# A head's fourth key and query class, the root of one column, and the last row in halves: three small edits to a hybrid decoder block

## The chip, the cores and the metric

The kernel runs on one core of a Trainium2 chip. The metric is device time in microseconds of one execution, the median of several. The engines are named as in the profile: PE (matrix multiply) with its weight loads, DVE (vector), ACT (activations and copies), POOL (elementwise work on a second vector engine) and SP, whose queue issues most DMAs. Every engine works through its instructions in order and waits on semaphores for the others.

## The reference, cut to what matters

One decoder layer on a sequence of 2048 positions with width 1024: an adaptive RMS norm, one wide input projection, two branches in parallel (a gated linear recurrence and a dilated attention), a gated merge, an output projection, and a last RMS norm. The part that the change touches is the attention and the last norm:

```python
DILATED_GROUPS = ((128, 1), (512, 4), (2048, 16))      # window, dilation; 8 heads of width 128
for window, dilation in DILATED_GROUPS:
    o, l = dilated_window_attention(q, k, v, window, dilation)   # banded softmax over strided keys
    outs.append(o); lses.append(l)
w = jax.nn.softmax(jnp.stack(lses, axis=0), axis=0)    # the three mixed by their denominators
o = jnp.einsum("gbsh,gbshd->bshd", w, jnp.stack(outs, axis=0))
...
x = x + gate[:, None, :] * (merged @ w_o[l])
return rms_norm(x, g_final)                            # x * rsqrt(mean(x*x) + 1e-6) * g
```

All matrix products are computed in three passes: each operand is split into a high part (rounded) and a low part (the rest), and high times high, high times low and low times high are summed. A split is therefore two instructions: a copy that rounds (mostly ACT, line 160) and a subtraction that gives the rest (POOL, line 166, or DVE, line 169).

## The kernel before, in words

The program runs in stages: input projections with a Strassen scheme (to about 1340 us), the attention together with the projections of the branches' outputs (about 1350 to 1866 us), the rest of these projections (to about 1965 us and on), and the output projection with the last norm (from about 2010 us).

**Attention.** The sequence is handled in two halves of 1024 positions (`f`), and each half has eight heads; I number these 16 in program order from 0 to 15. Positions are sorted by their remainder modulo 4 into four classes. A head has six units of work, `ORDER`: class 0, window part 0, class 1, window part 1, class 2, class 3. A class unit takes the queries of one class against the keys of the same class; a window unit takes the queries of 512 neighbouring positions, which are spread over all four classes.

Time is laid out in slots, one unit of scores in each (lines 1881 to 1906). A slot has five places: HEAD, the scores and their softmax, SOFTMAX, two thirds of the slot's filling work, EXCHANGE, the last third, WEIGHTS, the transposes of the unit seven slots back, then the sums of the unit eight slots back, TAIL. The filling work (`fill`) is the matrix product of the branches' outputs, some 2.8 steps of three 512-column matmuls for each slot, so that PE has work while the softmax goes on. The order in which the instructions are written is the order in which each engine runs them (`manual_schedule`); what stands at a place is put there by `at(slot, place, function)`.

For a head that starts in slot B, `Head.enlist` (line 1696) sets these steps, as far as they matter here:

- `load_kq` (line 1418), one DMA on SP's queue for each class, 256 KB in the first half and 384 KB in the second, into one of four buffers `kraw`: classes 0 and 1 in slot B-5, class 2 in B-4, class 3 in B-3, all at TAIL. For the first head all four are loaded in slot -5.
- `split_kq` (line 1425): ACT writes the high half into `KQ[:, 0, c]`, POOL the low half into `KQ[:, 1, c]` (DVE for classes 0, 1 and 3 of the first head). `KQ` has one buffer, so the split of a class has to follow the last scores of the head before that read it. Class 0 is split at B-2 HEAD, class 1 at B-2 SOFTMAX, class 2 at B-1 HEAD, class 3 at B HEAD. The scores of class 3 of the head before stand in slot B-1.
- `window_queries` (line 1430): POOL copies the queries of a window part, high and low, from all four classes into the order of the window unit (tile `q1`; its rows read `CAST q<-kq`). Part 0 at B HEAD, for the scores in slot B+1; part 1 at B+1 EXCHANGE.
- `gather` (line 1626) at B-1 WEIGHTS, for the head before: four small ACT instructions that spread that head's softmax statistics; then `exchange` (line 1633), one small PE product of these (row `sc<-sm,msk`) in the middle of the scores of slot B; then `maxima` on DVE, `exponentials` on ACT, and `weights` on DVE at B WEIGHTS, whose result `M` scales the exponentials on ACT (line 1542) ahead of the transposes, from slot B+1 on.
- `split_v` and `split_v1` (lines 1446 and 1463): the values of an older head, high on ACT, low on POOL, at TAIL; that of the class 3 unit stands at B-1 TAIL.

**The end.** The output projection handles the rows in eight pairs of blocks (`output_pair`, line 2085), each with seven products; two rows of 128 positions come out of a pair, and each is normalised: square sums on ACT (`square`, line 2018), the root by `rstd_first` and `rstd_last` or `mean_first`, `mean_last` and `rstd_last`, then a scale and a store. `rstd_last` (line 176) takes the reciprocal of ACT's square root and improves it by one Newton step, five DVE instructions on a tile of 128 x 1 in this stage (128 x 4 elsewhere). In the last pair the gain has been multiplied in before; the second row is scaled whole on ACT (line 2141) and stored by one DMA of 512 KB, just ahead of the first row's last product (`last_output`, line 2045), whose square sum, root, scaling in two halves (ACT and DVE) and two DMAs of 256 KB end the program.

Of the kernel before, what the change touches and what calls it, by code (L numbers as in the profile page):

```python
# [14 lines left out]
AF = mybir.ActivationFunctionType  # L15
ALU = mybir.AluOpType
# [9 lines left out]
CH = 512  # L26
# [64 lines left out]
def decoder_block(ctx, tc, x, c, positions, g_norm, w_mod, b_mod, w_in, b_gate, conv_w, conv_b,  # L91
                  w_a, b_a, w_x, b_x, lam, w_out_rnn, w_out_attn, w_o, g_final, cst, out):
    nc = tc.nc
    cnt = [0]

    def T(pool, shape, dt, tag, **kw):
        cnt[0] += 1
        return pool.tile(shape, dt, tag=tag, name=f"{tag}_{cnt[0]}", **kw)
# [72 lines left out]
    def rstd_first(ss):  # L171

        nc.vector.tensor_scalar(ss[:, 0], ss[:, 0], 1.0 / D, EPS, ALU.mult, ALU.add)
        nc.scalar.activation(ss[:, 1], ss[:, 0], AF.Sqrt)

    def rstd_last(ss):
        v, y, t = (ss[:, i] for i in range(3))
        nc.vector.reciprocal(y, y)
        nc.vector.tensor_tensor(t, y, y, ALU.mult)
        nc.vector.tensor_tensor(t, t, v, ALU.mult)  # L180
        nc.vector.tensor_scalar(t, t, -0.5, 1.5, ALU.mult, ALU.add)
        nc.vector.tensor_tensor(y, y, t, ALU.mult)

    def rstd(ss):
        rstd_first(ss)
        rstd_last(ss)
# [348 lines left out]
    outv = out[0].rearrange("(n j r) d -> n r j d", n=NB, r=4)  # L535
# [167 lines left out]
    with tc.manual_schedule():  # L703
# [35 lines left out]
        nc.tensor.transpose(pt[:, :N_PAR], prow[:N_PAR, :], ident[:N_PAR, :N_PAR])  # L739
        nc.vector.tensor_copy(par[:], pt[:, :N_PAR])  # L740
        rstd_last(norm[0])
        scale_dve(1)
        sums(0, 1)
# [417 lines left out]
    for t in range(6):  # L1161
        pieces = []
        i0 = t * P
        while i0 < (t + 1) * P:
            hd, i = divmod(i0, 96)
            n = min(96 - i, (t + 1) * P - i0)
# [156 lines left out]
    for f in range(2):  # L1323
# [20 lines left out]
        n = 0  # L1344
# [55 lines left out]
    HEAD, SOFTMAX, EXCHANGE, WEIGHTS, TAIL = range(5)  # L1400
    plan, due = {}, []

    def at(slot, place, fn, *args):
        plan.setdefault((slot, place), []).append((fn, args))
# [5 lines left out]
    class Head:  # L1410
# [283 lines left out]
                stored.add((self.f, self.h, i))  # L1694

        def enlist(self, B):
            for c, (ld, s, place) in enumerate(((5, 2, HEAD), (5, 2, SOFTMAX), (4, 1, HEAD), (3, 0, HEAD))):
                at(B - (ld if B else 5), TAIL, self.load_kq, c)
                at(B - s, place, self.split_kq, c)
            at(B, HEAD, self.window_queries, 0)  # L1700
            at(B + 1, EXCHANGE, self.window_queries, 1)
            e = B + NU
            at(e - 1, WEIGHTS, self.gather)
            at(e, HEAD, due.append, self.exchange)
            at(e, SOFTMAX, self.exchange_alone)
            at(e, SOFTMAX, self.maxima)
            at(e, SOFTMAX, self.exponentials)
            at(e, WEIGHTS, self.weights)
            for u, (kind, x) in enumerate(ORDER):
                s = B + u + LAG  # L1710
                at(s - 1, TAIL, self.scale, kind, x)
                at(s - 1, TAIL, self.split_v if kind == "c" else self.split_v1, x)
                at(s - 3, TAIL, self.load_v if kind == "c" else self.load_v1, x)
            e = B + NU + LAG
            at(B + LAG - 1, TAIL, self.load_gate)
            at(e, TAIL, self.merge, 1)
            at(e + 1, TAIL, self.merge, 3)
            at(e + 2, TAIL, self.store)
# [209 lines left out]
    v = {}  # L1928
# [78 lines left out]
    XO, SS = {}, {}  # L2007
# [7 lines left out]
    def cols(p, i, j):  # L2015
        return XO[p, i][:, j * CH : (j + 1) * CH]

    def square(p, i, js=(0, 2)):
        if (p, i) not in SS:
            SS[p, i] = T(up[0], [P, 3, 1], F32, "ss", bufs=4)  # L2020
        jk = T(up[0], [P, D], BF16, "jk", bufs=1)
        c = slice(js[0] * CH, js[1] * CH)
        nc.scalar.activation(jk[:, c], XO[p, i][:, c], AF.Square, accum_out=SS[p, i][:, 2 if js == (0, 1) else 0])
# [10 lines left out]
    def product(p, i, ps, b, first, last):  # L2034
        bh, bl = B[b]
        s = ops.pop(7 * p + i)
        for k in range(KH):
            mm3(ps[:], s[:, 0, k, :], s[:, 1, k, :], bh[:, k, :], bl[:, k, :],
                first=first and k == 0, last=last and k == KH - 1, skip_group_check=True)
        n_p[0] += 1  # L2040

    def new_sum(tag):
        return T(px_, [P, CH], F32, tag, bufs=1 + (tag == "X"))

    def last_output(p):
        u2, V = psum.pop(p)
        product(p, 6, V, "B22", False, True)
        tt(cols(p, 0, 1), V[:], cols(p, 0, 1), ALU.add)
        if p == NP - 1:
            square(p, 0, (1, 2))  # L2050
            tt(cols(p, 0, 0), cols(p, 0, 0), v["gf"][:, :CH], ALU.mult)
            mean_last(SS[p, 0], 0, 2)
            n, r = divmod(2 * p, 4)
            rstd_last(SS[p, 0])
            y = SS.pop((p, 0))[:, 1]
            nc.scalar.activation(cols(p, 0, 0), cols(p, 0, 0), AF.Copy, scale=y)
            nc.scalar.dma_start(outv[n, r, :, :CH], cols(p, 0, 0))
            nc.vector.scalar_tensor_tensor(cols(p, 0, 1), cols(p, 0, 1), y, v["gf"][:, CH:], ALU.mult, ALU.mult)
            nc.sync.dma_start(outv[n, r, :, CH:], cols(p, 0, 1))
            return  # L2060
        n = n_p[0]
        on_p(n + 1, square, p, 0)
        on_p(n + 2, lambda: rstd_first(SS[p, 0]))
        on_p(n + 3, finish_row, p, 0)

    def mean_first(ss, i):
        nc.vector.tensor_scalar(ss[:, i], ss[:, i], 1.0 / D, EPS, ALU.mult, ALU.add)

    def mean_last(ss, i, j):
        nc.vector.scalar_tensor_tensor(ss[:, 0], ss[:, i], 1.0 / D, ss[:, j], ALU.mult, ALU.add)  # L2070
        nc.scalar.activation(ss[:, 1], ss[:, 0], AF.Sqrt)

    def last_gain(p, j):
        nc.gpsimd.tensor_tensor(cols(p, 1, j), cols(p, 1, j), v["gf"][:, j * CH : (j + 1) * CH], ALU.mult)
# [3 lines left out]
    def on_p(n, fn, *args):  # L2078
        after.setdefault(n, []).append((fn, args))

    def fire_p():
        for fn, args in after.pop(n_p[0], ()):
            fn(*args)

    def output_pair(p):
        def add_x(i, j, u):
            nc.gpsimd.tensor_tensor(cols(p, i, j), cols(p, i, j), u[:], ALU.add)

        X = new_sum("X")
        product(p, 0, X, "B11", True, False)  # L2090
        fire_p()
        if p:
            last_output(p - 1)
            fire_p()
        Z = new_sum("Z")
        product(p, 1, Z, "T2", True, True)
        u1 = T(up[0], [P, CH], F32, "u1")
        u2 = T(up[0], [P, CH], F32, "u2", bufs=2)
        u3 = T(up[0], [P, CH], F32, "u3")
        nc.scalar.activation(u1[:], X[:], AF.Copy)  # L2100
        tt(u2[:], Z[:], u1[:], ALU.add)
        fire_p()
        W_ = new_sum("W")
        product(p, 2, W_, "T3", True, True)
        tt(u3[:], W_[:], u2[:], ALU.add)
        add_x(1, 1, u3)
        add_x(0, 1, u2)
        fire_p()
        V = new_sum("V")
        psum[p] = u2, V  # L2110
        product(p, 3, V, "T1", True, False)
        tt(cols(p, 1, 1), V[:], cols(p, 1, 1), ALU.add)
        add_x(1, 0, u3)
        if p == NP - 1:
            square(p, 1, (1, 2))
            last_gain(p, 1)
        fire_p()

        def row_start():
            product(p, 4, X, "B21", False, True)  # L2120
            tt(cols(p, 0, 0), X[:], cols(p, 0, 0), ALU.add)

        if p < NP - 1:
            row_start()
            fire_p()
        Y = new_sum("Y")
        product(p, 5, Y, "T4", True, True)
        tt(cols(p, 1, 0), Y[:], cols(p, 1, 0), ALU.add)
        n = n_p[0]
        if p == NP - 1:  # L2130
            fire_p()
            square(p, 1, (0, 1))
            last_gain(p, 0)
            mean_first(SS[p, 1], 0)
            row_start()
            fire_p()
            mean_last(SS[p, 1], 2, 0)
            square(p, 0, (0, 1))
            rstd_last(SS[p, 1])
            mean_first(SS[p, 0], 2)  # L2140
            nc.scalar.activation(XO[p, 1][:], XO[p, 1][:], AF.Copy, scale=SS.pop((p, 1))[:, 1])
            n, r = divmod(2 * p, 4)
            nc.sync.dma_start(outv[n, r + 1], XO[p, 1][:])
            last_output(p)
            return
        on_p(n + 1, square, p, 1)
        on_p(n + 2, lambda: rstd_first(SS[p, 1]))
        on_p(n + 3, finish_row, p, 1)
        fire_p()

    LAST = 3 * KT * KT
    with tc.manual_schedule():
# [34 lines left out]
        for p in range(NP):  # L2187
            output_pair(p)
# [31 lines left out]
```

## Time and profile before

| | |
|---|---|
| median of 3 runs | 2163.99 us (2163.35 to 2165.45) |
| the profiled execution's own time | 2165.13 us |
| its span, first to last instruction | 2163.4 us |
| PE busy | 2137.6 us, 99% |
| DVE, ACT, POOL busy | 69%, 60%, 51% |
| granted PE clock, mean | 0.998 |

The profile is of one execution. A row of the instructions in order of time gives the start in us, the duration in us, engine, line, operation, the tiles written and read (`out<-in`), shape and number; in brackets stands how long the engine was idle before and what it waited for, as inferred from semaphores. Rows of neighbouring instructions of one kind are merged (`x2`, `x12`); the duration is then that of the whole row. The end of a matmul is modelled, so PE can look busy across short gaps. A line in the list of waits reads: engine, tile and line that waited, what it waited for, total us, number, longest.

### The profile page before, as it was taken

Reading aid. Unit: us, or ns where it says so; the run is one execution under the profiler, and the core shown is the slowest. Engines: PE = TensorE matmul, PEld = TensorE weight load, DVE = VectorE, ACT = ScalarE, POOL = GpSimd, SP = SyncE. Lnnn points to the kernel's source line nnn. Section 1 sums busy time; section 2 is a strip of 40 time slices with the busy share of each in tenths; the row PEclk is TensorE's granted clock in tenths of the full one; section 3 lists DMA queues with packets and bytes.
Section 4 is the critical chain, followed back from the end, with each engine's and each line's share of the span. In section 5 each row is a group of like instructions: output and inputs, shape, how many; then the busy total and the mean of one; then the engine's idle time right before and its main releaser. Section 6 shows DMA issues by size and latency. Waiting matters only on the chain.

```text
span 2163.4 us, 32584 instructions
## 1 busy us (share of the span) xinstructions
PE 2137.6 (99%) x10538; PEld 1788.5 (83%) x10539; DVE 1487.2 (69%) x2606; ACT 1296.6 (60%) x2591; POOL 1109.5 (51%) x868
## 2 busy tenths in 40 slices
PE   9999999999999999999999999999999999999998
PEld 6888778888888888888888887888888988878886
DVE  6759878768656725545436675587777787788887
ACT  5748668668644527457547532677888877443333
POOL 1467667777666323223223574466666564422544
PEclk9999999999999999999999999999999999999999
DMA  8467887886655378898996666988887776898553
GB/s 302 143 210 258 279 291 264 285 296 240 175 113 165 108 237 290 296 311 307 324 321 228 161 166 183 295 271 262 277 265 242 238 246 216 300 320 292 180 173 110
DMA packets 416431, 521.39 MB, mean 241 GB/s; under 512 B 107558, under 2 KB 282882, under 8 KB 415236
## 3 DMA queue, kind: packets, MB, share of 16 engines
q1 hardware_dynamic: 376244, 401.65, 59.8%
q10 hardware_dynamic: 34384, 99.78, 12.1%
q0 software_dynamic: 5632, 17.88, 2.5%
q8 instruction: 83, 1.36, 0.2%
q14 instruction: 88, 0.72, 0.1%
HBM read 332.02 MB, written 187.17 MB: 240 GB/s over the span
## 4 chain that ended last, share of the span: by engine, by line
PE 68%; DVE 6%; DMA 3%; issue 2%; POOL 1%; ACT 1%; SPq 0%; POOLq 0%; ACTq 0%; DVEq 0%
PE X L152 13%; PE V L152 13%; PE pj L152 9%; PE Z L152 7%; PE W L152 7%; PE Y L152 6%; PE sc L152 4%; PE o L152 4%; PE pg L152 1%; DMA fg<-mrT 1%; PE pT L1562 1%; PE pT L1575 1%; DMA fg<-gaT 1%; DVE ptl L169 1%; DMA meT<-fg 1%
## 5 line engine op out<-in xcount | busy, mean ns | idle before, releaser
L166 POOL TENSOR_TENSOR S<-R,S 128x512 fp32r<-128x512 f32 x192 | 294.5, 1542 | 169.8 <-ACT S L160 82.6
L152 PE MATMUL V<-T,S 128*128 128x512 f32 x1344 | 324.3, 390 | 1.9 <-DVE ev L455 1.9
L152 PE MATMUL X<-T,S 128*128 128x512 f32 x1344 | 323.9, 390 | 1.5 <-ACT u L385 1.2
L152 PE MATMUL pj<-yh,S 128*128 128x512 f32 x896 | 321.9, 403 | 0.7 <-DVE S L169 0.6
L152 PEld LDWEIGHTS X<-T,S 128*128 128x128 f32 x1344 | 251.7, 188 | 56.5 <-ACT u L385 2.8
L152 PEld LDWEIGHTS V<-T,S 128*128 128x128 f32 x1344 | 251.9, 188 | 55.9 <-issue 1.7
L166 POOL TENSOR_TENSOR S<-s,S 128x512 fp32r<-128x512 f32 x116 | 170.7, 1472 | 150.5 <-ACT S L160 114.0
L152 PEld LDWEIGHTS pj<-yh,S 128*128 128x128 f32 x896 | 168.5, 188 | 32.0 <-DVE S L169 1.9
L152 PE MATMUL pj<-yl,S 128*128 128x512 f32 x448 | 176.0, 393 | 1.2 <-POOL yl L166 1.0
L1475 ACT ACTIVATE pp<-pp,st 128x256 f32<-128x256 f32 (+3 forms) x256 | 133.7, 523 | 71.3 <-DVE st L1474 70.3
L160 ACT ACTIVATE S<-s 128x512 fp32r<-128x512 f32 x124 | 77.3, 623 | 145.2 <-DVE s L285 88.2
L152 PE MATMUL W<-T,S 128*128 128x512 f32 x672 | 161.6, 389 | 0.0
L152 PE MATMUL Y<-T,S 128*128 128x512 f32 x672 | 161.5, 389 | 0.0
L152 PE MATMUL Z<-T,S 128*128 128x512 f32 x672 | 161.4, 389 | 0.0
L160 ACT ACTIVATE S<-R 128x512 fp32r<-128x512 f32 x200 | 121.5, 622 | 59.1 <-DMA R<-in_w_in_dram 15.0
L169 DVE TENSOR_TENSOR ptl<-pT,pth 128x384 fp32r<-128x384 f32 (+1 forms) x160 | 97.8, 628 | 74.3 <-ACT pth L160 72.1
L152 PEld LDWEIGHTS W<-T,S 128*128 128x128 f32 x672 | 126.0, 188 | 26.9 <-issue 0.9
L152 PEld LDWEIGHTS Z<-T,S 128*128 128x128 f32 x672 | 126.1, 188 | 26.2
L152 PEld LDWEIGHTS Y<-T,S 128*128 128x128 f32 x672 | 126.1, 188 | 26.2
L974 DVE SCALAR_TENSOR_TENSOR xc<-xr,par,xc 128x512 f32<-128x512 f32 x96 | 103.9, 1082 | 53.2 <-ACT xc L968 51.0
L166 POOL TENSOR_TENSOR s<-R,s 128x512 fp32r<-128x512 f32 x32 | 43.4, 1357 | 187.2 <-ACT s L160 158.2
L1542 ACT ACTIVATE pp<-pp,M 128x256 f32<-128x256 f32 (+3 forms) x256 | 118.0, 523 | 21.0 <-DVE M L1674 21.0
(417 smaller groups left out, 4920.5 us busy)
## 6 DMA issues: line engine op xcount, KB each, us to landing
sD<-S ACTq DMA_DIRECT2D x140, 512.0 KB, 3.7
S<-sD SPq DMA_DIRECT2D x140, 512.0 KB, 5.3
S<-wD SPq DMA_DIRECT2D x82, 512.0 KB, 5.4
R<-in_w_in_dram SPq DMA_DIRECT2D x144, 256.0 KB, 3.4
wD<-s ACTq DMA_DIRECT2D x64, 256.0 KB, 5.1
kraw<-kqT SPq DMA_DIRECT2D x32, 384.0 KB, 5.1
T<-in_w_mod_dram SPq DMA_DIRECT2D x16, 512.0 KB, 9.1
vN<-ev SPq DMA_DIRECT2D x32, 256.0 KB, 2.7
```

Of the source, the lines that this page charges most:

```text
L152: nc.tensor.matmul(o, lhsT=l, rhs=r, start=st, stop=sp, **kw)
L160: nc.scalar.activation(o, i, AF.Copy)
L166: nc.gpsimd.tensor_tensor(o, i, h.bitcast(F32), ALU.subtract)
L169: return nc.vector.tensor_tensor(o, i, h.bitcast(F32), ALU.subtract).ins
L974: nc.vector.scalar_tensor_tensor(xc, xr[:, i : i + CH], cw(i), xc, ALU.mult, ALU.add)
L1475: nc.scalar.activation(pdst, pdst, AF.Exp, bias=m_, scale=-1.0, accum_out=l_)
L1542: nc.scalar.activation(pp, pp, AF.Copy, scale=w)
L1562: nc.tensor.transpose(pt[:, c0 + j * P : c0 + (j + 1) * P], pp[i][:, k * P : (k + 1) * P], ident)
L1575: nc.tensor.transpose(pt[:, c * P : (c + 1) * P], pp[:, half * P : (half + 1) * P], ident)
```

## The change

Three edits. First, the fourth class (c = 3) is loaded at B-4 TAIL instead of B-3 TAIL, behind class 2, and split at B-1 EXCHANGE instead of B HEAD. The first head's load stays where it is, and its split moves past no other instruction of its engines. For every other head the split's ACT half moves ahead of the last third of slot B-1's fill, the `gather` of the head before, the copy of the class 2 unit's transposed probabilities, the scaling of the class 3 unit and its `split_v`; the POOL half moves ahead of what the last third of the fill has for POOL and of the low half of `split_v`.

Second, `rstd_last` on a single column does `t = y * y * v` in one instruction whose two factors are column scalars, and the last product with a column scalar: four DVE instructions instead of five.

Third, in the last pair the second row is scaled and stored in halves by `put`: the half with columns 512 to 1023 where the whole row stood, the other inside `last_output`, behind `mean_last` of the first row and ahead of its `rstd_last`.

```diff
     def rstd_last(ss):
         v, y, t = (ss[:, i] for i in range(3))
         nc.vector.reciprocal(y, y)
-        nc.vector.tensor_tensor(t, y, y, ALU.mult)
-        nc.vector.tensor_tensor(t, t, v, ALU.mult)
+        if y.shape[1] == 1:
+            nc.vector.tensor_scalar(t, y, y, v, ALU.mult, ALU.mult)
+        else:
+            nc.vector.tensor_tensor(t, y, y, ALU.mult)
+            nc.vector.tensor_tensor(t, t, v, ALU.mult)
         nc.vector.tensor_scalar(t, t, -0.5, 1.5, ALU.mult, ALU.add)
-        nc.vector.tensor_tensor(y, y, t, ALU.mult)
+        if y.shape[1] == 1:
+            nc.vector.tensor_scalar(y, y, t, None, ALU.mult)
+        else:
+            nc.vector.tensor_tensor(y, y, t, ALU.mult)
...
-            for c, (ld, s, place) in enumerate(((5, 2, HEAD), (5, 2, SOFTMAX), (4, 1, HEAD), (3, 0, HEAD))):
+            for c, (ld, s, place) in enumerate(((5, 2, HEAD), (5, 2, SOFTMAX), (4, 1, HEAD), (4, 1, EXCHANGE))):
                 at(B - (ld if B else 5), TAIL, self.load_kq, c)
                 at(B - s, place, self.split_kq, c)
...
-    def last_output(p):
+    def last_output(p, between=None):
...
             mean_last(SS[p, 0], 0, 2)
+            between()
             n, r = divmod(2 * p, 4)
             rstd_last(SS[p, 0])
...
-            nc.scalar.activation(XO[p, 1][:], XO[p, 1][:], AF.Copy, scale=SS.pop((p, 1))[:, 1])
             n, r = divmod(2 * p, 4)
-            nc.sync.dma_start(outv[n, r + 1], XO[p, 1][:])
-            last_output(p)
+            y = SS.pop((p, 1))[:, 1]
+
+            def put(j):
+                nc.scalar.activation(cols(p, 1, j), cols(p, 1, j), AF.Copy, scale=y)
+                nc.sync.dma_start(outv[n, r + 1, :, j * CH : (j + 1) * CH], cols(p, 1, j))
+
+            put(1)
+            last_output(p, lambda: put(0))
             return
```

## The prediction

> **What bounds the kernel now.** I read the busy times first, then the windows by stage, the list of who waited for whom, and last the instructions in order of time around the places that the change touches.
>
> ```profile
> PE 2137.6 (99%) x10538; PEld 1788.5 (83%) x10539; DVE 1487.2 (69%) x2606; ACT 1296.6 (60%) x2591; POOL 1109.5 (51%) x868
> ```
>
> ```profile
> 1866.00:1965.00 99.00, 97.52 (x424) 78.77 (x423) 84.83 (x135) 43.62 (x76) 30.60 (x51) 1.00 0.93 321
> ...
> 2010.00:2155.00 145.00, 145.00 (x640) 119.78 (x638) 123.51 (x207) 51.75 (x107) 68.87 (x47) 1.00 0.43 150
> ```
>
> TensorE (PE) fills the span. The columns after the window are its length and the busy time of PE, weight load, VectorE (DVE), ScalarE (ACT) and GpSimd (POOL), then the granted clock, the DMA share and GB/s. In the output stage (from 2010 us) PE never idles, so what DVE saves there before the last pair is worth nothing. A gain must come from PE idle time in the attention stage (about 1350 to 1866 us) or from the tail behind the last matmul. The weight loads' waits name one cause in attention:
>
> ```profile
> PEld sc L152 <- POOL q L1436: 5.6, 8, 2.1
> ```
>
> These are the window scores waiting for the permuted queries, which POOL copies behind the split of the fourth key and query class. Heads are numbered 0 to 15 in program order. How long PE loses is read against head 13, which does not wait:
>
> ```profile
> 1730.95 0.27 PE L152 MATMUL o<-pth,vh 128*128 128x128 f32 x1
> ...
> 1732.55 0.39 PE L152 MATMUL pj<-yh,S 128*128 128x512 f32 x1
> ...
> 1733.94 0.93 PE L1562 MATMUL pT<-cs,pp 128*128 128x128 f32 x7
> ```
>
> From the last product in front of the window scores to the fill behind them 1.60 us pass; the six fill matmuls up to the transposes take 1.39 us, 0.23 each. So the transposes start 2.29 us after that last product with three fill matmuls between (heads 10 and 14) and 2.99 with six (head 15).
>
> **Head 14, the largest loss.**
>
> ```profile
> 1757.05 0.96 ACT L1630 ACTIVATE sm<-st,cs 128x32 f32<-128x32 f32 x4
> ```
>
> ```profile
> 1757.40 1.87 POOL L166 TENSOR_TENSOR kq<-kraw,kq 128x768 fp32r<-128x768 f32 x1
> 1761.56 1.28 POOL L166 TENSOR_TENSOR yl<-R,yh 128x512 fp32r<-128x512 f32 x1 [2.28 <-DVE yh L1771]
> ...
> 1764.05 1.83 POOL L166 TENSOR_TENSOR kq<-kraw,kq 128x768 fp32r<-128x768 f32 x1
> 1765.82 1.68 POOL L1436 CAST q<-kq 128x512 fp32r<-128x512 f32 x2
> ```
>
> ```profile
> 1764.71 0.27 PE L152 MATMUL o<-pth,vh 128*128 128x128 f32 x1
> 1766.95 3.10 PE L152 MATMUL sc<-kq,q 128*128 128x256 f32 x12 [1.97 <-POOL q L1436]
> ...
> 1771.07 0.93 PE L1562 MATMUL pT<-cs,pp 128*128 128x128 f32 x7
> ```
>
> ```profile
> 1766.90:1770.80 3.90, 3.75 (x15) 0.59 0.44 158
> ```
>
> Without a wait the transposes would start at 1764.71 + 2.29 = 1767.00; they start at 1771.07, 4.07 us late. About 2.1 us are the wait and its remainder, the rest a stretch at half clock right behind it (granted 0.59 over 3.9 us, so 0.41 x 3.9 = 1.6 us).
>
> The fourth class's low half is the POOL row at 1764.05. The change queues it behind the third's (1757.40, ends 1759.27), ahead of the fill's split at 1761.56, in a gap of 2.28 us; 1.83 us fit. Its ACT half then stands ahead of the row at 1757.05 and is done by 1757.9. The value split keeps its time, so the copies start at 1764.05 instead of 1765.82. The pair takes 1.2 to 1.7 us; PE wants the first at 1764.8 and the second a quarter us later, so about 0.25 us of wait stay.
>
> Late next are the transposes: they need the exponentials scaled by this head's weights.
>
> ```profile
> 1765.01 1.42 DVE L169 TENSOR_TENSOR yl<-R,yh 128x512 fp32r<-128x512 f32 x1
> ```
>
> ```profile
> 1768.05 1.23 ACT L1542 ACTIVATE pp<-pp,M 128x384 f32<-128x384 f32 x2 [2.54 <-DVE M L1674]
> ```
>
> Both scalings are now done at 1769.28, hidden by the stall. DVE's 1.42 us ran out just behind POOL's split (1764.05 + 1.83); the weights and the scaling, 1.6 us after that, queue behind it. With POOL's split gone from there I take all of this 1.1 us sooner, both scalings done at 1768.2. The second transpose moves from 1771.17 to about 1768.25: gain 2.9 us. Bounds: 1.2 us where the run had no slow stretch anyway and M doesn't move, 4.1 if nothing takes the wait's place.
>
> [...]
>
> **Head 10, where the move itself costs.**
>
> ```profile
> 1621.90 0.96 ACT L1630 ACTIVATE sm<-st,cs 128x32 f32<-128x32 f32 x4
> 1622.77 0.95 ACT L160 ACTIVATE pth<-pT 128x512 fp32r<-128x512 f32 x2
> ...
> 1624.74 0.62 ACT L160 ACTIVATE vh<-vraw 128x512 fp32r<-128x512 f32 x1
> 1625.26 0.84 ACT L160 ACTIVATE kq<-kraw 128x768 fp32r<-128x768 f32 x1
> ```
>
> ```profile
> 1623.37 1.16 DVE L169 TENSOR_TENSOR ptl<-pT,pth 128x512 fp32r<-128x512 f32 x2 [1.76 <-ACT pth L160]
> ```
>
> ```profile
> 1623.24 0.38 PE L152 MATMUL sc<-sm,msk 128*128 128x128 f32 x2
> ...
> 1628.24 0.27 PE L152 MATMUL o<-pth,vh 128*128 128x128 f32 x1
> ...
> 1633.44 0.87 PE L1562 MATMUL pT<-cs,pp 128*128 128x128 f32 x6 [0.27 <-ACT pp L1542]
> ```
>
> The ACT half (1625.26) moves ahead of the gather (1621.90). Back to back, an ACT instruction follows 0.10 us before the one ahead of it ends (1624.74 + 0.62 against 1625.26), so the insert is 0.84 - 0.10 = 0.74 us; for heads 1 to 7, with two thirds of the columns, I estimate 0.53. Behind it stand the gather, on which PE's exchange waits, and the probabilities' copy, for which DVE already idles 1.76 us. The exchange at 1623.24 has 0.38 us to spare: new wait 0.4. DVE, in order, is 0.74 us later from 1623.37 on, up to the weights. PE arrives at the transposes early, since the copies no longer stop it (1628.24 + 2.29 + 0.4 = 1630.9), but the scaled exponentials set them (the wait in the last row), and those come 0.5 later, a little of the 0.74 coming back where POOL is free. Loss 0.5 us, bounds +0.75 and -1.2 (all of the query wait recovered).
>
> **The other heads.**
>
> ```profile
> 1797.20 0.49 PE L152 MATMUL sc<-sm,msk 128*128 128x128 f32 x2 [0.26 <-ACT sm L1630]
> ...
> 1802.31 0.27 PE L152 MATMUL o<-pth,vh 128*128 128x128 f32 x1
> ...
> 1806.66 0.93 PE L1562 MATMUL pT<-cs,pp 128*128 128x128 f32 x7
> ```
>
> ```profile
> 1404.54 1.25 PEld L152 LDWEIGHTS sc<-kq,q 128*128 128x128 f32 x10 [0.19 <-POOL q L1436]
> ```
>
> ```profile
> 1374.17 0.96 ACT L1630 ACTIVATE sm<-st,cs 128x32 f32<-128x32 f32 x4
> ```
>
> ```profile
> 1376.05 0.39 PE L152 MATMUL sc<-sm,msk 128*128 128x128 f32 x2
> ```
>
> Head 15: 1806.66 - 1802.31 - 2.99 = 1.36 us late; the copies' wait goes, the exchange, already waiting, gets the whole 0.74: gain 0.6 (0 to 1.4). Heads 2 (its row is shown), 5 and 6 lose about 0.2 each to the copies; 2 and 5 give 0.3 together; 6, whose transposes follow its weights closely, loses as much by the ACT insert: 0 (0.4 either way). Elsewhere the exchange has 0.9 us or more in hand, more than the insert; head 1 has the least (1376.05 - 1374.17 - 0.96). The load moved ahead on SP's queue has its buffer free three slots before, and lands in two and a half slots instead of two; the value load that it overtakes has two slots until its split: 0 (0 to 0.5).
>
> Attention: 2.9 - 0.5 + 0.6 + 0 = 3.0 us. Behind it, at 0.93 of the DMA engines and 321 GB/s, transfers could eat part of a head start: I take back 0.3 (0 to 1).
>
> **The tail.**
>
> ```profile
> 2133.61 0.15 DVE L181 TENSOR_SCALAR ss<-ss 128x1 f32<-128x1 f32 x1
> 2133.80 1.03 DVE L182 TENSOR_TENSOR ss<-ss 128x1 f32<-128x1 f32 x1
> ...
> 2154.12 0.73 DVE L179 TENSOR_TENSOR ss<-ss 128x1 f32<-128x1 f32 x1
> ...
> 2155.40 0.68 DVE L2048 TENSOR_TENSOR xo<-V,xo 128x512 f32<-128x512 f32 x1
> ```
>
> ```profile
> 2155.51 1.15 ACT L2141 ACTIVATE xo<-xo,ss 128x1024 f32<-128x1024 f32 x1 [1.00 <-POOL xo L2074]
> 2156.56 0.61 ACT L2023 ACTIVATE jk<-xo 128x512 bf16<-128x512 f32 x1
> ```
>
> ```profile
> 2133.51 1.30 POOL L166 TENSOR_TENSOR S<-s,S 128x512 fp32r<-128x512 f32 x1
> ```
>
> ```profile
> 2154.64 0.39 PE L152 MATMUL V<-B22h,S 128*128 128x512 f32 x1
> ```
>
> The second row's scale (1.15 us) blocks the last square sum, whose input is there at 2155.40 + 0.68 = 2156.08. In halves, the first is done before, the second runs beside the short DVE chain of the first row's root. The merged operation with two column scalars is not in the trace. Its bounds are the two-tensor product beside POOL (0.73 and 1.03 us) and the operation with one tensor and two constants, which took 0.15 us while POOL's 1.30 us ran (2133.61); I take the second, as it too streams one tensor. So DVE is free before the last matmul ends (2155.03), and the add starts 0.1 behind that instead of at 2155.40; the square follows at 2155.9 instead of 2156.56: 0.65 us. The root's own chain is one operation (0.19, from 2133.61 to 2133.80) shorter. Together 0.84 us; 0.4 if the merged operation stalls like the product, 0.2 if besides the extra half DMA queues in front of the last.
>
> **Sum.** The profiled execution took 2165.13 us (span 2163.4, 1.7 around it), 1.1 more than the median of the three runs, 2163.99. 2165.13 - 3.0 + 0.3 - 0.84 = 2161.6 us. A run without the slow stretch starts about 1.6 lower and gains that much less, so the forecast stands for both.
>
> **Rivals.** (1) Full recovery: the weights don't set the transposes at 10 and 14. Query waits 1.6 (head 10) + 4.1 + 1.4 + 0.4 = 7.5, less 0.4 + 0.74 for the exchanges and 0.25 left at head 14, so 6.1, and 0.84: 2158.2. For it: at head 14 the scalings were done 1.8 us before the transposes came; against: head 10 waits there already. (2) A slow stretch remains. Either it has another cause than the gap and stays, or it moves: at head 10 PE now waits in one piece, from 1630.9 to past 1633.3, longer than the gap at 14, and the clock halves there. Either way 1.6 us come back: 2163.2. For it: the window after head 14's gap; against: it is the only such window of this profile, so its condition is known from one case. (3) Slower: the ACT insert stands in front of the gather in all 15 later heads, 7 x 0.53 + 8 x 0.74 = 9.6 us if every exchange waits in full: 2165.13 + 9.6 - 0.84 - 3.0 = 2170.9. It decides from the point where ACT reaches the gather 1 us later than in the trace; the 0.9 us and more of slack speak against it. That the copies come no sooner would need POOL or ACT blocked at the new place; at head 14 POOL's gap of 2.28 us is empty, so this has no chance of its own (2164.3 without the 3.0 and the 0.3).
>
> **Chances.** Forecast 0.45, full recovery 0.2, remaining stretch 0.27, slower 0.08. A difference of 0.2% (4.3 us) is about what a measurement here can tell from none; the line for faster is 2159.7. Rival 1 and the low end of the forecast lie below it: faster 0.3; slower beyond 2168.3 only rival 3: 0.07; same 0.63. Range 2158.2 (rival 1) to 2164.9 (rival 2 with head 14's lower bound).
>
> **What would show it.** After: the query waits of PE near 0 at heads 10, 14, 15; POOL's fourth kq ahead of the value split; granted clock 1.00 behind head 14; new or longer waits "sm" at 10 and 15 and "pp" at 10; the last square sum starting 0.8 us after the last matmul's end rather than 1.5. Wrong if the copies still hold PE, if "sm" waits appear at many heads, or if stage 1866 to 1965 grows by more than 1 us.

## The result and the profile after

The changed kernel takes 2161.18 us, the median of 22 executions (2158.21 to 2164.91), beside 2163.93 us for the kernel before on the same chip (22 executions, 2162.30 to 2166.19). The ratio is 0.9987, 95% interval 0.9981 to 0.9993: 2.8 us faster, about two thirds of the 0.2% from which the prediction would speak of a difference. The forecast was 2161.6 us. The profiled execution took 2161.23 us, 3.90 less than that of before, which lay 1.2 us above its median.

The busy times after, then windows of 100 us from the attention stage: two of before, the same two of after, and the stage behind it after. The columns are as in the prediction; the granted clock is the third number from the right.

```profile
PE 2136.6 (99%) x10539; PEld 1788.3 (83%) x10539; DVE 1463.3 (68%) x2582; ACT 1296.2 (60%) x2592; POOL 1120.6 (52%) x868
```

```profile
1600.00:1700.00 100.00, 98.02 (x645) 88.44 (x645) 77.88 (x206) 83.29 (x206) 65.33 (x51) 1.00 0.75 233
1700.00:1800.00 100.00, 97.68 (x632) 88.14 (x631) 78.91 (x193) 80.49 (x203) 62.92 (x49) 0.98 0.79 249
```

```profile
1600.00:1700.00 100.00, 97.55 (x633) 88.14 (x632) 75.10 (x201) 82.32 (x206) 65.22 (x51) 0.98 0.73 230
1700.00:1800.00 100.00, 99.63 (x657) 89.81 (x656) 77.52 (x204) 83.37 (x209) 66.51 (x51) 1.00 0.78 253
...
1866.00:1965.00 99.00, 97.68 (x427) 79.54 (x427) 84.56 (x135) 42.00 (x74) 29.34 (x52) 1.00 0.95 331
```

Between 1700 and 1800 us, where head 14 stands, PE has 2 us less idle time and the full clock. Between 1600 and 1700, where head 10 stands, it has become worse, and the lowered clock is now there. The list of waits shows that one wait has taken the place of another; the first line is of before, the others of after.

```profile
PE sc L152 <- POOL q L1436: 4.0, 4, 2.0
```

```profile
PE pT L1568 <- ACT pp L1548: 2.9, 4, 2.1
PEld sc L152 <- POOL q L1442: 0.2, 1, 0.2
```

PE no longer waits for POOL's query copies, apart from 0.2 us at its weight loads. It waits for ACT's scaled exponentials instead (2.9 us in all, where it was 0.8 before), 2.1 us of it in one piece, at head 10. In order of time, there (lines of the attention are 6 higher than before):

```profile
1631.07 1.27 POOL L166 TENSOR_TENSOR yl<-R,yh 128x512 fp32r<-128x512 f32 x1 [2.17 <-DMA vraw<-vN]
1631.18 1.18 DVE L1678 TENSOR_TENSOR M<-M,t__3081_16167 128x16 f32<-128x16 f32 x1
...
1633.61 0.30 PE L1568 MATMUL pT<-cs,pp 128*128 128x128 f32 x1 [2.09 <-ACT pp L1548]
1634.18 0.87 PE L1568 MATMUL pT<-cs,pp 128*128 128x128 f32 x6 [0.27 <-ACT pp L1548]
```

```profile
1633.00:1638.00 5.00, 4.12 (x22) 3.77 (x22) 3.59 (x12) 3.96 (x12) 3.28 (x4) 0.75 0.10 35
```

The granted clock of 0.75 over 5 us is a stretch at half clock, as it stood behind head 14 before; in the trace it reaches from 1635.50 to 1638.92. Next the transposes of heads 11, 14 and 15, and the tail:

```profile
1669.32 0.93 PE L1568 MATMUL pT<-cs,pp 128*128 128x128 f32 x7
...
1769.99 0.87 PE L1568 MATMUL pT<-cs,pp 128*128 128x128 f32 x6 [0.27 <-ACT pp L1548]
...
1804.01 0.93 PE L1568 MATMUL pT<-cs,pp 128*128 128x128 f32 x7
...
2151.24 0.39 PE L152 MATMUL V<-B22h,S 128*128 128x512 f32 x1
2152.45 0.63 ACT L2029 ACTIVATE jk<-xo 128x512 bf16<-128x512 f32 x1 [0.54 <-DVE xo L2054]
2153.83 0.27 DVE L180 TENSOR_SCALAR ss<-ss 128x1 f32<-128x1 f32 x1
2154.33 0.21 DVE L186 TENSOR_SCALAR ss<-ss 128x1 f32<-128x1 f32 x1
2154.58 0.75 DVE L2065 SCALAR_TENSOR_TENSOR xo<-xo,ss,gf 128x512 f32<-128x512 f32 x1
```

And of before, head 11's transposes and the last scaling:

```profile
1667.26 0.93 PE L1562 MATMUL pT<-cs,pp 128*128 128x128 f32 x7
...
2158.70 0.75 DVE L2058 SCALAR_TENSOR_TENSOR xo<-xo,ss,gf 128x512 f32<-128x512 f32 x1
```

Each term of the forecast can now be measured, as what its place adds to the distance between the two profiles (positive is a gain, us; up to head 1 the two differ by 0.04):

| place | forecast | measured |
|---|---|---|
| heads 1 to 9 (head 9's transposes, 1598.69 against 1598.25) | 0 | -0.44 |
| head 10, the wait (second transpose 1634.18 against 1633.44) | -0.5 | -0.30 |
| half-clock stretch behind head 10 (by head 11, 1669.32 against 1667.26) | only in rival 2 | -1.32 |
| head 14 (second transpose, 1769.99 against 1771.17) | 2.9 | 3.24 |
| head 15 (1804.01 against 1806.66) | 0.6 | 1.47 |
| from there to the last matmul (2151.24 against 2154.64) | -0.3 | 0.75 |
| last matmul's end to last scaling (2.95 against 3.67) | 0.84 | 0.72 |
| last scaling to the kernel's end (6.65 against 6.43) | 0 | -0.22 |
| sum | 3.5 | 3.90 |

These are single executions. The 0.75 of the stage to the last matmul need not be the change's: of the four versions below that leave the split in its old place, three gain there too (the load alone 0.77, the third edit alone 1.04, the second edit alone 0.49).

### The profile page after: what moved, and what is told of

Its sections match the earlier page's. It is cut to its first block, busy times and chain, and to the rows that moved or that the text cites. A ratio compares the mean times of both kernels' runs of the same rounds, so it can differ in the third digit from the quotient of the medians.

```text
span 2159.4 us, 32571 instructions
## 1 busy us (share of the span) xinstructions
PE 2136.6 (99%) x10539; PEld 1788.3 (83%) x10539; DVE 1463.3 (68%) x2582; ACT 1296.2 (60%) x2592; POOL 1120.6 (52%) x868
## 4 chain that ended last, share of the span: by engine, by line
PE 71%; DVE 4%; DMA 3%; issue 1%; POOL 1%; ACT 1%; SPq 0%; ACTq 0%; POOLq 0%; DVEq 0%
PE X L152 14%; PE V L152 13%; PE pj L152 12%; PE Z L152 7%; PE W L152 7%; PE Y L152 6%; PE sc L152 4%; PE o L152 4%; PE pg L152 1%; PE pT L1568 1%; PE pT L1581 1%; DMA fg<-gaT 1%; DMA kraw<-kqT 1%; DVE ptl L169 1%; DVE yl L169 1%
```

## The experiments

The question behind all of them: the sum came out nearly as forecast, but rival 2's condition came true in the profile as well. So: is the attention gain really the move of the split, what is the new wait made of, does the half-clock stretch follow the gap, and which edit shortens the tail? Where an experiment leaves out the second edit, the lines of the attention are again those of before.

**The split and load alone.** The kernel before with the first edit only.

```diff
-((5, 2, HEAD), (5, 2, SOFTMAX), (4, 1, HEAD), (3, 0, HEAD))
+((5, 2, HEAD), (5, 2, SOFTMAX), (4, 1, HEAD), (4, 1, EXCHANGE))
```

> The kernel before with the first edit alone (load and split of the fourth class sooner); roots and halves as before. Theory (the move gives the whole gain in attention, the roots and halves only the 0.7 us behind the last matmul): PE's waits for the copied queries go at heads 10, 14 and 15, the wait of the transposes at head 10 grows from 0.6 to 2 us, the last matmul ends 3 to 3.5 us before the one of the kernel before, and the median lies 2 us below it, 0.7 above the changed kernel. Rival (the roots in the output stage, by less work on DVE, give part of it): the last matmul ends less than 2 us sooner.

Measured: 2161.68 us (2159.88 to 2165.22), ratio 0.9985 (0.9976 to 0.9993). One line of the waits and the row at head 10:

```profile
PE pT L1562 <- ACT pp L1542: 2.6, 3, 2.1
```

```profile
1634.08 2.11 PE L1562 MATMUL pT<-cs,pp 128*128 128x128 f32 x7 [2.09 <-ACT pp L1542]
```

The last matmul starts at 2151.20, as in the changed kernel (2151.24), and its end is followed by the tail of before: 3.65 us to the last scaling. So the whole of the change in PE's time is this edit, and the roots are worth nothing inside the output stage, as forecast. The 0.7 us by which the median was to lie above the changed kernel's can't be seen in the times.

**The load alone**, moved to B-4 with the split where it was.

```diff
-((5, 2, HEAD), (5, 2, SOFTMAX), (4, 1, HEAD), (3, 0, HEAD))
+((5, 2, HEAD), (5, 2, SOFTMAX), (4, 1, HEAD), (4, 0, HEAD))
```

> The kernel before with only the load of the fourth class one slot sooner, its split where it was. Theory (the load is off the path in both places): within 1 us of the kernel before, PE's waits for the copied queries as before (4.0 us, longest 2.0) with the slow stretch behind head 14. Rival (the load was late, and the split waited for it): the waits for the copied queries shrink as in the changed kernel.

Measured: 2164.11 us, ratio 0.9998 (0.9989 to 1.0007), and the copies' wait is 4.0 us, 4 times, as before. With the split in its old place, the load is off the path.

**The split behind the transposes.** In the changed kernel, at a new place behind the transposes of slot B-1, so with the ACT half no longer ahead of the gather and of the probabilities' copy.

```diff
...
+            run(s, TURNED)
...
-(4, 1, EXCHANGE)
+(4, 1, TURNED)
```

> The changed kernel with the fourth class's split set behind the transposes of slot B-1 instead of at its EXCHANGE, so that on ACT it follows the gather and the copy of the transposed probabilities; the load stays sooner. Theory (the ACT half ahead of these makes DVE and the weights late): DVE's wait for that copy at head 10 goes back from 2.35 to 1.8 us, the exchanges at heads 10 and 15 wait no longer for the gather than before, the weights of head 10 come 0.5 to 0.7 sooner, and the median is 0.5 to 2 us below the changed kernel's, the larger if the slow stretch goes. Rival (the weights are late by the fill's splits ahead of them on DVE, whatever ACT does): the transposes at head 10 wait 2 us as in the changed kernel, and the median is the same within 0.5 us.

Measured: 2159.53 us (2156.34 to 2161.31), ratio 0.9972 (0.9963 to 0.9981). Head 10 in this run:

```profile
1630.09 1.28 POOL L166 TENSOR_TENSOR yl<-R,yh 128x512 fp32r<-128x512 f32 x1 [1.28 <-DVE yh L1777]
1630.20 1.20 DVE L1678 TENSOR_TENSOR M<-M,t__3081_16167 128x16 f32<-128x16 f32 x1
...
1632.64 0.30 PE L1568 MATMUL pT<-cs,pp 128*128 128x128 f32 x1 [1.63 <-ACT pp L1548]
```

```profile
1632.00:1637.00 5.00, 4.09 (x27) 3.72 (x28) 3.62 (x12) 3.96 (x12) 3.24 (x4) 1.00 0.26 98
```

DVE's wait for the copy of the probabilities, 2.35 us in the changed kernel, is back at the 1.76 of before, and the gap is 1.63 us instead of 2.09. The insert on ACT thus lengthened the gap, but did not make it: 1.63 us remain. The clock behind it stays at 1.00 in this execution; whether the shorter gap is the reason is not shown, as the last section tells. Heads 1 to 9 gain 0.41 us here (the transposes are 0.48 us later than those of before at head 1, and 0.07 at head 9), where the changed kernel lost 0.4.

**The weights sooner.** In the changed kernel, `weights` right behind the exponentials.

```diff
-            at(e, WEIGHTS, self.weights)
+            at(e, SOFTMAX, self.weights)
```

> The changed kernel with the weights computed right behind the exponentials of the exchange (place SOFTMAX of the slot) instead of at WEIGHTS, so ahead of the fill's splits on DVE. Theory (the late weights set the transposes at head 10, and the gap they leave brings the half clock): the transposes' wait for the scaled exponentials goes from 2.9 us to under 0.5, no slow stretch before the end, and the median is 3 to 4 us below the changed kernel's, near 2157.5. Rival A (the slow stretch has another cause): the wait goes, the stretch stays, 2 us below. Rival B (DVE then idles for ACT's exponentials at every head, and its splits come late): other waits of PE grow and the median is the same or above.

Measured: 2158.97 us (2158.16 to 2164.21), ratio 0.9975 (0.9965 to 0.9985), less gain than the 3 to 4 us expected on top of the change. Head 10:

```profile
1628.57 0.17 DVE L1678 TENSOR_TENSOR M<-M,t__3076_16151 128x16 f32<-128x16 f32 x1
...
1631.90 0.96 PE L1568 MATMUL pT<-cs,pp 128*128 128x128 f32 x7 [0.56 <-DVE ptl L169]
```

The same product takes 0.17 us where it took 1.18 and 1.20: it now stands ahead of the fill's splits in DVE's order. The transposes' wait for the scaled exponentials is gone from PE's list; what remains at head 10 is 0.56 us for DVE's low half of the probabilities, which has taken its place, and the mean granted clock is 0.999, where the changed kernel's profile with its one stretch has 0.998. Part of the rival with other waits came as well: head 10's second transpose is 1.41 us ahead of the one of before, head 11's only 0.18. The 1.2 us go in small pieces, at the scores behind the transposes (0.26 us of waiting for DVE's statistics) and at the window unit's transposes.

**Both mends.** The two diffs above together.

> The changed kernel with both mends at once: the split of the fourth class behind the transposes of slot B-1, and the weights right behind the exponentials. Theory (both mends take away the same wait, that of head 10's transposes for the scaled exponentials, with the half-clock stretch behind it, so they do not add up; what is left to gain is the lateness of heads 1 to 9, some 0.4 us, and the 0.4 us that head 15 waits): ratio to the kernel before 0.9968 to 0.9973, about 2157.5 to 2158.5 us, no PE wait of 1 us or more in the attention. Rival (two separate causes, whose gains of 1.65 and 2.2 us on the changed kernel add): about 2155.5 us or less, ratio 0.996. Rival 2 (with the weights early nothing depends on the split's place): as with the early weights alone, 2159, ratio 0.9975.

Measured: 2159.59 us (2158.74 to 2162.33), ratio 0.9974 (0.9965 to 0.9984). Two separate causes whose gains add (0.996) are ruled out. Between the theory (0.9968 to 0.9973) and the rival that nothing depends on the split's place once the weights are early (0.9975) the time cannot decide. In the profile the transposes of head 15 are 5.98 us ahead of before, against 5.05 with the split behind the transposes and 4.33 with the early weights. But this execution came to head 1 already 1.08 us ahead, that of the early weights 0.52 ahead, that of the other mend 0.48 behind. From head 1 on they gain 4.90, 3.81 and 5.53 us: both mends together are not ahead of the split alone. From head 15 to the last matmul 0.86 us were lost again (5.12 ahead), where the early weights alone gained 1.38 (5.71 ahead). What sets this stage to the us is not settled by these runs; the head start alone does not.

**The weights alone**, in the kernel before.

> The kernel before with one edit: the weights stand right behind the exponentials, no split or load moved, roots and last row as before. Theory (before the change the window copies, not the weights, hold PE at head 14): the query copies' wait stays at 4 us in all with about 2 at head 14, the half-clock stretch stays behind it, and the time is that of the kernel before within 1 us: 2163.0 to 2164.5, ratio 0.9995 to 1.0003; at head 10 the transposes come up to 0.3 us sooner. Rival (the late weights set the transposes in the kernel before, too, and the move of the split was not needed): 2 us or more faster, 2162 or less, ratio 0.999 or less.

Measured: 2164.09 us, ratio 0.9999 (0.9989 to 1.001).

```profile
PE sc L152 <- POOL q L1436: 3.0, 3, 1.5
```

```profile
1769.00:1773.00 4.00, 3.73 (x23) 2.84 (x24) 3.86 (x11) 1.85 (x4) 1.61 (x2) 1.00 0.52 181
```

The theory holds: without the move the copies still hold PE, and early weights gain nothing. One detail fell: at head 14 the gap was 1.52 us and no stretch followed, though the theory expected 2 us with the stretch behind it.

**The third edit alone**, the halves with the root in five operations.

> The third edit alone: the last pair's second row scaled and stored in halves, the root in five operations as before, the split and the load as before. Theory (the ACT instruction of 1.15 us that scaled the second row held up the last square sum): from the last matmul's end to the start of the last scaling 3.0 us instead of 3.67, the square sum starting about 0.85 us behind that matmul's end; all waits of PE as in the kernel before; time 2163.3 us. Rival (the products of column by column stall beside POOL, so that DVE comes late to the last add and the merged operations were needed for it): 3.3 to 3.6 us, time within 0.3 us of the kernel before.

Measured: 2164.01 us, ratio 0.9996 (0.9987 to 1.0005). The rival holds: 3.29 us to the last scaling. The tail, and the window behind head 14's gap:

```profile
2152.10 0.39 PE L152 MATMUL V<-B22h,S 128*128 128x512 f32 x1
...
2152.96 0.72 ACT L2146 ACTIVATE xo<-xo,ss 128x512 f32<-128x512 f32 x1 [1.01 <-POOL xo L2075]
2153.63 0.63 ACT L2023 ACTIVATE jk<-xo 128x512 bf16<-128x512 f32 x1
```

```profile
1766.70:1770.70 4.00, 3.88 (x25) 3.41 (x26) 3.43 (x15) 2.87 (x8) 1.61 (x2) 1.00 0.46 155
```

**The second edit alone**, the root in four operations; one execution.

> The second edit alone: the root of one column in four operations. Theory (in the profile of the changed kernel the two operations with column scalars took 0.27 and 0.21 us, the three that they replace 0.15 to 0.16 each and a start apart, so a chain of 0.95 instead of 0.97 us): from the last matmul's end to the last scaling 3.6 to 3.7 us as before, the square sum 1.5 us behind that matmul, PE's waits as before, no difference in the time. Rival (the forecast's, one operation less, 0.19 us): 3.48 us; or, if the stalls of the products beside POOL had held up the last add, 3.3 us or less.

The tail's rows:

```profile
2160.22 0.39 PE L152 MATMUL V<-B22h,S 128*128 128x512 f32 x1
2160.16 1.15 ACT L2147 ACTIVATE xo<-xo,ss 128x1024 f32<-128x1024 f32 x1 [0.41 <-issue]
2160.64 0.69 DVE L2054 TENSOR_TENSOR xo<-V,xo 128x512 f32<-128x512 f32 x1 [0.50 <-PE V L152]
2161.43 0.63 ACT L2029 ACTIVATE jk<-xo 128x512 bf16<-128x512 f32 x1
2163.55 0.72 ACT L2062 ACTIVATE xo<-xo,ss 128x512 f32<-128x512 f32 x1 [0.98 <-DVE ss L186]
```

The theory written down fell, and the second rival holds: 2.94 us, the whole gain of the tail, without the halves. The second row's root is ready early, so ACT's 1.15 us starts 0.45 us before the last matmul ends, instead of 0.48 behind, and is over when the last square sum's input comes. (This one execution took 2169.99 us; it was 6.1 us late before head 1, in stages that the edit leaves alone, where the gaps of 2.48 and 3.10 us of the last section lie.)

**Early weights, whole last row.** The best of these parts: the kernel with early weights, less the third edit.

> The kernel with the early weights, less the third edit: the last pair's second row is again scaled whole and stored by one DMA; the root stays in four operations. Theory (with the merged root DVE is free when the last matmul ends and ACT scales the second row before the last square sum is wanted; the halves then save nothing and put one more DMA ahead of the last ones): the last square sum 0.82 us behind the last matmul's end and the last scaling 2.94 us behind it, as in halves; from the start of the last scaling to the kernel's end 6.44 instead of 6.62 us; so the tail is 0.2 us shorter, about 2158.8 us beside a kernel before of 2164.5, ratio 0.9974 (0.9965 to 0.9983); no PE wait of 1 us or more in the attention. Rival (the halves are needed together with the merged root): 3.3 us or more from the last matmul's end to the last scaling.

Measured: 2160.28 us (2159.43 to 2164.47), ratio 0.9985 (0.9976 to 0.9994). Its profile has the tail as expected, 2.95 us and then 6.43; the time missed the ratio of 0.9974 that was expected. The 0.2 us can't be seen in it, and it gains less than the early weights with halves (0.9975, 0.9965 to 0.9985), with intervals that overlap. The profiled execution lost its time far away from the edit:

```profile
301.11 3.32 PE L152 MATMUL V<-T,S 128*128 128x512 f32 x7 [3.61 <-DVE ev L461]
```

```profile
301.00:306.00 5.00, 4.89 (x12) 3.86 (x13) 3.85 (x5) 3.53 (x6) 2.44 (x2) 0.50 0.70 266
```

The tails side by side, in us from the last matmul's end (its start plus 0.39), from the same rows of each run:

| kernel | roots | last row | last square sum | last scaling | from there to the end | sum |
|---|---|---|---|---|---|---|
| before | 5 | whole | 1.53 | 3.67 | 6.43 | 10.10 |
| third edit alone | 5 | halves | 1.14 | 3.29 | 6.61 | 9.90 |
| second edit alone | 4 | whole | 0.82 | 2.94 | 6.44 | 9.38 |
| changed | 4 | halves | 0.82 | 2.95 | 6.65 | 9.60 |
| early weights, whole row | 4 | whole | 0.82 | 2.95 | 6.43 | 9.38 |

The roots bring 0.72 us and the halves 0.20; with the roots in place the halves cost 0.22, all of it behind the last scaling. There the five profiles with halves take 6.60 to 6.65 us and the six without 6.43 to 6.48; why is not shown.

Of the four versions with a mend, three are the fastest of all: 2158.97, 2159.53 and 2159.59 us, ratios 0.9972 to 0.9975. Their intervals lie clear of 1 and touch that of the changed kernel at the edge only (0.9981 to 0.9985). The fourth, the early weights with the whole last row, has 0.9985 and is no better than the changed kernel (0.9987). So the mends are likely, not certainly, worth about 2 us.

## Why the prediction was right, and where it was not

**Head 14**: right in mechanism and size. The copies no longer hold PE, the clock stays up, and the second transpose gains 3.24 us (forecast 2.9). The move of the split does it: alone it brings all of PE's gain, while the load alone and the early weights alone leave the copies' wait (4.0 and 3.0 us) and the time as it was. What comes late next is what the prediction said, the scaled exponentials: the bracket of the row at 1769.99 names them. (These scale the head before with its own weights; the prediction's "this head's weights" names the wrong head, which changes no number.) The reason for the earlier weights holds too: DVE's 1.42 us, now clear of POOL's split, take 0.75.

```profile
1767.05 0.75 DVE L169 TENSOR_TENSOR yl<-R,yh 128x512 fp32r<-128x512 f32 x1
```

**Head 10**: the transposes' wait took the place of the copies' wait, as forecast, and the loss by the wait was 0.30 instead of 0.5. The new wait for the exchange, priced at 0.4, was 0.10 us. PE's idle time hardly grew: it was 1.99 us before, in four pieces (0.63, 0.52, 0.57 and 0.27), and is 2.36 now, of which 2.09 in one. That the ACT insert makes the weights later is borne out by DVE's wait for the copy (1.76, 2.35, and 1.76 again with the split behind the transposes). Why they are late at all was not seen: one product of 128x16 takes 1.18 to 1.20 us beside a POOL subtraction and 0.17 without. In the changed kernel both end within 0.03 us of each other (1631.18 + 1.18 against 1631.07 + 1.27). It was as slow in the kernel before, so it explains the wait and not what the change added to it:

```profile
1630.43 1.20 DVE L1672 TENSOR_TENSOR M<-M,t__3081_16175 128x16 f32<-128x16 f32 x1
```

**The half-clock stretch**: here the forecast's sum failed and rival 2 was right. It let the stretch vanish; the profiled execution has it behind head 10, 1.32 us. Rival 2 named that place and the reason, a gap there as long as head 14's had been (2.09 us here, 1.97 there). Going by the mean granted clocks (last section), about half of the 22 executions have no stretch at all, so the step failed in at most the other half; in which of those the stretch lies at head 10 is open.

**Head 15**: mis-sized, 1.47 for 0.6. The prediction charged the exchange with the full 0.74 of the ACT insert. But ACT was waiting for DVE's softmax statistics there (3.04 us before, 1.78 in the changed kernel), and these came sooner, because a DVE product that had taken 1.45 us took 0.69 (first row before, second after):

```profile
1792.17 1.45 DVE L1791 TENSOR_TENSOR fg<-fg,fg 128x512 f32<-128x512 f32 x1
```

```profile
1791.05 0.69 DVE L1797 TENSOR_TENSOR fg<-fg,fg 128x512 f32<-128x512 f32 x1
```

**Heads 1 to 9**: forecast 0, measured -0.44, at the lower bound that the prediction gave for heads 2, 5 and 6; the run with the split behind the transposes shows that it is the place of the split (+0.41 there). **The load**: 0, as forecast. **The stage to the last matmul**: a take-back of 0.3 was forecast, 0.75 was gained; the runs range from -0.86 to 1.38 here, and those with the split in its old place gain up to 1.04, so neither number can be put down to the change.

**The tail**: right in size (0.72 for 0.84, less 0.22 at the end), wrong in the step. The prediction held that the last square sum could come 0.65 us sooner only with both the halves, which free ACT, and the merged operation, which frees DVE, and gave 0.19 to one operation less. In fact the merged operation does it alone, and not by being one fewer: 0.27 and 0.21 us stand for three products of 0.16, so the last chain is just 0.02 shorter. What it does is not to stall beside POOL. Before, products of 128x1 took 1.21, 1.02 and 0.73 us in the last 7 us of PE's work, each until a POOL instruction ended, and DVE came late to the last add. In the changed kernel the merged operations take 0.27 and 0.21 there while POOL runs, and DVE has time to wait for PE (1.17 us at the row of 2148.95). First before, then after:

```profile
2148.26 1.21 DVE L180 TENSOR_TENSOR ss<-ss 128x1 f32<-128x1 f32 x1
...
2149.70 1.02 DVE L182 TENSOR_TENSOR ss<-ss 128x1 f32<-128x1 f32 x1
```

```profile
2142.25 3.79 POOL L2094 TENSOR_TENSOR xo<-xo,u 128x512 f32<-128x512 f32 x3 [6.84 <-DVE ss L173]
...
2144.37 0.27 DVE L180 TENSOR_SCALAR ss<-ss 128x1 f32<-128x1 f32 x1
...
2144.86 0.21 DVE L186 TENSOR_SCALAR ss<-ss 128x1 f32<-128x1 f32 x1
...
2148.95 0.69 DVE L2128 TENSOR_TENSOR xo<-X,xo 128x512 f32<-128x512 f32 x1 [1.17 <-PE X L152]
```

The prediction took that from the operation with two constants, rightly, though with 0.15 for what measures 0.27. It did not follow where the second row's scale on ACT starts once DVE is free: 0.45 us before the last matmul ends, so that the whole row no longer blocks the square sum and the halves are not needed.

So the time came out within 0.4 us of the forecast, in part because errors cancelled: the stretch and heads 1 to 9 took 1.8 us more than the sum held, head 15 and the stage behind gave 1.9 more. That part is luck. **Rival 1** did not come, since the weights did set the transposes at 10 and 14. **Rival 3** did not come: exchange waits stay below 0.5 us.

## What to carry to other kernels

When a wait is removed, look at the next one in line at every head, and at how the idle time is spread: at head 10 nearly the same idle time (2.36 us for 1.99), 2.09 of it in one gap instead of four smaller ones, had a stretch at half clock behind it that cost another 1.3 us in the profiled execution. A tiny DVE product on a critical chain was better kept off POOL's busy time here (0.16 us alone, up to 1.23 beside POOL), by its form (a column scalar instead of a second tensor) or by its place in the order; the first was worth 0.7 us in the tail here, the second about 2 us of the whole in two of three versions that had it. When two profiles are compared stage by stage, take off what one was ahead before the stage. Test edits that come in one change one by one: of three, one brought the attention's gain, one the tail's, and the third cost 0.2 us once the second was there.

## What the runs showed of the hardware

**Tiny DVE products beside POOL.** The root's products of 128x1 took 0.15 to 0.16 us where no POOL instruction ran and up to 1.23 beside one; the weights' operation of 128x16 (`M<-M,t_`) took 0.17 and up to 1.25. Of these two kinds, 33 begin while POOL runs in the profiles of before and after, and each ends 0.01 to 0.09 us behind the end of POOL's instruction. The root's scalar operation with two columns, on the other hand, took 0.26 to 0.28 us with POOL running and without, and a product with one operand in PSUM took 0.17 us at 1764.13 before, inside POOL's 1.83 us. What holds the first two up is not shown.

**When the clock fell.** Take every gap of PE of at least 1 us that the eleven profiles list behind a named wait, apart from the first microseconds. Ten gaps of 1.97 to 3.61 us (1.97 four times, 2.09 twice, 2.48, 2.53, 3.10, 3.61) were followed by a stretch at half clock in nine cases; the exception is a gap of 1.97, in the third edit alone. None of the seventeen of 1.00 to 1.63 us was.

How the exception differs can be read in part. Before, the granted clock is halved at 1767.57 us, full again at 1770.98, and halved again at 2160.10, behind the last matmul: 3.41 us at half clock, then 389.12 at full. In the changed kernel the same changes stand at 1635.50, 1638.92 and 2154.33: 3.41 us, then 515.41. PE's idle time is compared in windows as long as these stretches. First the window ahead of the stretch before, and the stretch; then the two windows that share the spared gap in the third edit alone:

```profile
1764.15:1767.57 3.42, 1.36 (x11) 1.01 (x9) 3.32 (x8) 1.10 (x3) 3.35 (x3) 1.00 0.66 195
1767.57:1770.98 3.41, 3.41 (x13) 3.17 (x14) 2.94 (x12) 2.93 (x8) 1.10 (x1) 0.50 0.31 118
```

```profile
1762.38:1765.79 3.41, 2.38 (x18) 2.05 (x16) 3.27 (x11) 2.50 (x7) 3.41 (x4) 1.00 0.28 92
1765.79:1769.20 3.41, 2.38 (x15) 2.09 (x16) 3.31 (x11) 1.37 (x3) 1.48 (x2) 1.00 0.81 266
```

Two gaps of 1.97 us: one leaves PE 2.06 us idle in the window ahead of the stretch, the other 1.03 in each of two. In the changed kernel the window ahead of the stretch (1632.09 to 1635.50) has 1.79 us of idle time. With such windows laid end to end, forward and back from the stretch, no other that ends before the last matmul does has more than 1.33 in these two profiles (296.42 to 299.83 before). That the idle time within one such window decides is the author's reading; these runs do not show it. Behind the gaps of 3.10 and 3.61 us the granted clock is 0.50 over 5 us (300 to 305 in the second edit alone, 301 to 306 with early weights and the whole row), so those two stretches are longer than 3.41 us.

So a gap of about 2 us was followed by the stretch in one execution and not in another. The gap of 1.63 us of the split behind the transposes had the clock at 1.00 behind it; whether that is due to its length one profile does not tell. The mean granted clocks fit: the five profiles with 0.998 have a stretch each, and two of those with 0.999, the third edit alone and the split behind the transposes, have 1.00 behind the gaps of 1.97 and 1.63 us. Of the 22 executions of the changed kernel 11 have 0.999 (2160.2 us on average), 7 have 0.998 (2161.8) and 4 have 0.997 (2162.9). With the split behind the transposes 3 of 9 have 0.999, with the early weights 6 of 9. The wait named `V <- DVE ev` near 300 us was 0.5 to 3.6 us long from one execution to another, and where it was 2.53 us (the weights alone), 3.10 and 3.61, the clock behind it was halved too (0.66 over 300 to 305 us in the first, 0.50 in the others).
